# Two decoder layers on one core: high-part and low-part matmuls of a weight tile, k tile by k tile in place of one run after the other

## The chip, the cores and the metric

The kernel runs on one core of one Trainium2 chip. The metric is the device time of one execution in microseconds (us). The kernel before takes 2217.95 us, the median of three runs (2217.54 to 2218.45). A profile is one execution recorded by the hardware profiler; its times count from the start of the span, which is the time from the first to the last instruction.

## The reference

A trunk of two decoder layers works on 256 tokens of 2048 features, in float32:

```python
for layer in range(2):
    h = rmsnorm(x, mix_norm[layer])
    x = x + (sliding_window_attention(h, ...) if layer == 0 else rglru_block(h, ...))
    h = rmsnorm(x, ffn_norm[layer])
    x = x + conv_ffn(h, ...)
```

- Attention: 32 query heads and 8 key/value heads of 64, a window of 128, normed q and k, a learned sink in the softmax, then the output projection (2048 x 2048).
- RG-LRU: an input projection (2048 x 4096) into an x branch and a y branch; a causal convolution over 4 positions and block-diagonal gates (8 blocks of 256) on the x branch; a linear recurrence over the tokens; its result times gelu(y); the output projection (2048 x 2048).
- ConvFFN: `u = h @ w_up` (2048 x 12288), a causal convolution over 3 positions, `gelu(g) * v` of the two halves of `u`, and `@ w_down` (6144 x 2048). Both layers end with one; with their 288 of the 376 weight chunks they are most of the work.

## The kernel before, in words

**Layout.** Activations stay on chip, transposed: features on the 128 partitions, the 256 tokens along the free axis. `x` is the residual stream, `h` its normed form, in 16 "k tiles" of 128 features.

**Two parts of every operand.** A float32 number is split exactly into a high and a low part of type float32r. A product is hi*hi + hi*lo + lo*hi, accumulated in float32 in PSUM. With a weight's high part stationary, TensorE streams both parts of the activation, `[x_hi | x_lo]`, 512 columns; with its low part stationary, it streams `x_hi` alone, 256 columns, which are added to the second half of the same PSUM bank. So each k tile of each output tile needs one 512-column matmul (`mm_hi`, line 183) and one 256-column matmul (`mm_lo`, line 189), each with its own load of a 128 x 128 weight tile. Before the change `mm_hi` runs over all k tiles of an output tile first, and `mm_lo` after it.

**The stream of weights.** Weights come from HBM once, in 376 chunks of 1 MiB (128 x 2048), in the order of their use. Each has three buffers' worth of room at each stage: `raw` (as loaded), `hi` and `lo`. `advance()` (line 122) is called once per chunk, after that chunk's matmuls: it issues the transfer of a later chunk on SyncE's queue (line 102), has ScalarE cast a chunk's high part (line 109) and VectorE subtract to get its low part (line 117). A high buffer is free again when the last matmul that reads it is done, a raw buffer when the low split has read it.

**The stages, in order**, by the name of the PSUM tile:
- `pk`, `pv`, `pq`: the attention's projections. `attend()` weaves the steps of the attention between the high matmuls of a q tile.
- `po`: output projection, 16 output tiles. The first two go together, because the last two k tiles of `ao` come late; lines 605 to 608 run these k tiles alternately, high then low, one output tile after the other.
- `pu` and `pd`: the ConvFFN's up and down projection, in two halves of 24 pairs of `pu` tiles (one pair: a tile of `g` and one of `v`) and 8 pairs of `pd` tiles. One `pd` chunk holds 8 k tiles for two output tiles, so a run there has 8 matmuls, not 16.
- `px`, `py`: x and y branch of the RG-LRU's input projection, 20 and 12 output tiles. Behind `px` pairs follow the gate matmuls `g`. During `py`, the steps of the recurrence (`decay`, `coef`, `root`, `recur`, `proj`, `gated`, `zsplit`) are placed by hand on ScalarE, VectorE and GpSimd by the tables `before` and `after`; they produce `z`.
- `pr`: the RG-LRU's output projection from `z`, 16 output tiles; then the second ConvFFN.

**Late operands.** Where a stage's last two k tiles come late (the first pair of `pu`, `px` and `pr`), `late_pair()` (line 214) runs 14 k tiles of both output tiles first, then `mid()` (the norm's matmuls), then the last two.

**Epilogues.** Each is a generator, whose steps (`step(pend)`) are issued while the next tile's matmuls run: ScalarE copies one half of the bank, VectorE adds the other, and so on. PSUM has three double-bank buffers for these tiles.

**Order of the work.** All engines execute in the written order (a manual schedule); the waits between them follow from the tiles that they write and read.

Of the kernel before, what the change touches and what calls it, by code (L numbers as in the profile page):

```python
# [25 lines left out]
P = 128  # L26
D = 2048
T = 256
KD = D // P
# [11 lines left out]
def trunk(ctx, tc, xT, wq, wk, wv, wo, win, wg, wout, wup, wdn, mixg, ffng, kqg, sinks,  # L41
# [85 lines left out]
    def use():  # L127
        """The next chunk's parts."""
        c = st["use"]
        st["use"] += 1  # L130
        return his.pop(c), los.pop(c)
# [5 lines left out]
    def step(g):  # L137
        """Runs a generator to its next yield."""
        if g is not None:
            next(g, None)  # L140

# [1 line left out]
    def split_x(dst, src, gains, k):  # L143
        """dst[:, k] = the two parts of src * gain (src [P, T])."""
        act.activation(out=dst[:, k, 0, :], in_=src, func=AF.Copy, scale=gains[:, k:k + 1])
        dve.scalar_tensor_tensor(out=dst[:, k, 1, :], in0=src, scalar=gains[:, k:k + 1],
                                 in1=f(dst[:, k, 0, :]), op0=ALU.mult, op1=ALU.subtract)

    def stat(src, first):
        """sqa += src * src (src [P, 2, T])."""  # L150
        if first:
            pool.tensor_tensor(out=sqa, in0=src, in1=src, op=ALU.mult)
        else:
            pool.tensor_tensor(out=sqt, in0=src, in1=src, op=ALU.mult)  # L154
            pool.tensor_tensor(out=sqa, in0=sqa, in1=sqt, op=ALU.add)
# [5 lines left out]
    def rsqrt1(y, v):  # L161
        """A first guess of v ** -0.5."""
        act.activation(out=y, in_=v, func=AF.Ln)
        act.activation(out=y, in_=y, func=AF.Exp, scale=-0.5)

    def rsqrt2(y, v, tmp):
        """One Newton step towards v ** -0.5."""
        dve.tensor_tensor(out=tmp, in0=v, in1=y, op=ALU.mult)
        dve.scalar_tensor_tensor(out=tmp, in0=tmp, scalar=-0.5, in1=y, op0=ALU.mult, op1=ALU.mult)
        dve.scalar_tensor_tensor(out=y, in0=tmp, scalar=1.5, in1=y, op0=ALU.add, op1=ALU.mult)  # L170
# [20 lines left out]

    def x_epi(ps, d, n, gains, tp, out_=None, tag="xt"):
        """x's tiles d .. d + n take the product in ps [P, n, 512]; then h's, or the output's."""
        t = tp.tile([P, n, T], F32, tag=tag, name=f"xt{st['use']}")
        xs = x[:, d:d + n, :]
        for i in ([slice(0, n)] if out_ is None else [slice(i, i + 1) for i in range(n)]):
            dve.tensor_tensor(out=t[:, i], in0=ps[:, i, 0:T], in1=xs[:, i], op=ALU.add)  # L197
            dve.tensor_tensor(out=xs[:, i], in0=ps[:, i, T:], in1=t[:, i], op=ALU.add)  # L198
            if out_ is not None:
                nc.sync.dma_start(out=out_[:, d:d + n, :][:, i], in_=xs[:, i])  # L200
        if out_ is not None:
            return
        yield
        if gains is None:
            return
        for i in range(d, d + n):
            split_x(h, x[:, i, :], gains, i)
        yield
        if n == 2:
            stat(xs, d == 0)  # L210
        elif d % 2:
            stat(x[:, d - 1:d + 1, :], d == 1)

    def late_pair(ps, rhs, mid=None):
        """Two output tiles whose operand's last two k-tiles come late."""
        parts = [use(), use()]
        for i, (hi, lo) in enumerate(parts):
            mm_hi(ps[:, i], hi, rhs, rng(0, KD - 2))
            mm_lo(ps[:, i], lo, rhs, rng(0, KD - 2), stop=False)
        advance()  # L220
        if mid:
            mid()
        for i, (hi, lo) in enumerate(parts):
            mm_hi(ps[:, i], hi, rhs, rng(KD - 2, KD), start=False)
            mm_lo(ps[:, i], lo, rhs, rng(KD - 2, KD))
        advance()

    def softplus():
        """sp = softplus(-lam) = max(-lam, 0) + log1p(e), e = exp(-|lam|), by the series of
        log1p(e) = 2 artanh(z), z = e / (2 + e) <= 1/3."""  # L230
# [41 lines left out]
    # ================= attention =================  # L272
    with ExitStack() as ph:
# [35 lines left out]
        # key j of two blocks is seen from query i when i < j <= i + 128  # L309
# [69 lines left out]
        def kv_norm():  # L379
            """The first norm's factor along the free axis and along the partitions."""  # L380
            ps = psT.tile([P, 512], F32, tag="pT", name="pn")
            norm_pe(ps[:, 0:T])
            pc = psT.tile([P, 512], F32, tag="pT", name="pc")
            for b in range(2):
                for i in range(2):
                    pe.matmul(pc[:, b:b + 1], lhsT=sqa[:, i, b * P:(b + 1) * P], rhs=ones[:, 0:1],
                              start=i == 0, stop=i == 1)
            dve.tensor_scalar(out=cb, in0=ps[:, 0:T], scalar1=1.0 / D, scalar2=EPS, op0=ALU.mult, op1=ALU.add)
            dve.tensor_scalar(out=cb, in0=cb, scalar1=EPS, scalar2=None, op0=ALU.mult)
            dve.tensor_scalar(out=rcv, in0=pc[:, 0:2], scalar1=1.0 / D, scalar2=EPS, op0=ALU.mult, op1=ALU.add)  # L390
            dve.tensor_scalar(out=cc, in0=rcv.unsqueeze(2).to_broadcast([P, 2, 2]), scalar1=EPS, scalar2=None, op0=ALU.mult)
            rsqrt(rc, rcv, rct)
# [85 lines left out]
        def softmax(j, S):  # L478
            # column 2 * b + a: block b, head a
# [55 lines left out]
        def values(j):  # L535
# [3 lines left out]
            for b in range(2):  # L539
                # (key block, slice of the transposed probabilities)  # L540
# [15 lines left out]
        def attend(j, ps, hi, lo, rhs, nk):  # L556
            """One output tile's products over nk of its k-tiles; between them the steps of the
            attention of the query tiles j - 1 and j - 2."""
# [58 lines left out]
        for d in range(2, 16):  # L617
            hi, lo = use()
            ps = pj.tile([P, 512], F32, tag="pj", name=f"po{d}")
            mm_hi(ps, hi, ao, rng(0, KD))  # L620
            mm_lo(ps, lo, ao, rng(0, KD))
# [16 lines left out]
    # ================= ConvFFN =================  # L638
    def ffn(layer, nxt):
        with ExitStack() as ph:  # L640
# [29 lines left out]
            for half in range(2):  # L670
                for m in range(KH):
# [4 lines left out]
                    else:  # L676
                        for i in range(2):
                            hi, lo = use()
                            mm_hi(ps[:, i], hi, h, rng(0, KD))
                            mm_lo(ps[:, i], lo, h, rng(0, KD))  # L680
# [5 lines left out]
                for dp in range(8):  # L686
                    ps = mm.tile([P, 2, 512], F32, tag="mm", name=f"pd{layer}_{half}_{dp}")
                    for c in range(3):
                        hi, lo = use()
                        ks = [(kk, 8 * c + kk) for kk in range(8)]  # L690
                        for i in range(2):
                            mm_hi(ps[:, i], hi, g, ks, off=i * P, n=2 * P, start=c == 0)
                            mm_lo(ps[:, i], lo, g, ks, off=i * P, n=2 * P, stop=c == 2)
# [9 lines left out]
    # ================= RG-LRU =================  # L703
    with ExitStack() as ph:
# [6 lines left out]
        def projected(ps, n, eng):  # L711
            """A pair of output tiles: the two halves of the bank added, times the norm's factor."""
# [8 lines left out]
        with ExitStack() as px:  # L721
# [48 lines left out]
            def gates_rest(n, ps):  # L770
                """r (kept in a), i * x (in u), and t = tanh(4 sp r)."""
# [23 lines left out]
            for n in range(10):  # L795
# [3 lines left out]
                else:  # L799
                    rest = None  # L800
                    for i in range(2):
                        hi, lo = use()
                        mm_hi(ps[:, i], hi, h, rng(0, KD))
                        mm_lo(ps[:, i], lo, h, rng(0, KD))
# [21 lines left out]
        # a = exp(-8 sp r) = 1 - t (1 + a), and sqrt(1 - a a) = sqrt(t) (1 + a)  # L826
# [37 lines left out]
        # (n, i): what follows the products of tile i of the y projection's pair n, before the stream  # L864
        # moves on and after it
# [21 lines left out]
        for n in range(2, 8):  # L887
            ps = mm.tile([P, 2, 512], F32, tag="mm", name=f"py{n}")
            yps.append(ps)
            for i in range(2):  # L890
                hi, lo = use()
                mm_hi(ps[:, i], hi, h, rng(0, KD))
                mm_lo(ps[:, i], lo, h, rng(0, KD))
# [5 lines left out]
        for n in range(8):  # L899
# [7 lines left out]
            else:  # L907
                for i in range(2):
                    hi, lo = use()
                    mm_hi(ps[:, i], hi, z, rng(0, KD))  # L910
                    mm_lo(ps[:, i], lo, z, rng(0, KD))
# [12 lines left out]
def _layout(inp):  # L924
    import numpy as np

    def cols(w):
        """[K, N] -> [N / 128, 128, K / 128, 128]: chunk per 128 columns, rows on partitions."""
# [3 lines left out]
    def vec(v):  # L932
        """[..., n * 128] -> [128, ..., n]"""
# [49 lines left out]
```

## Time and profile before

| | |
|---|---|
| median of the runs | 2217.95 us (2217.54 to 2218.45) |
| span of the profiled execution | 2215.8 us |
| TensorE matmul (PE) busy | 2185.9 us, 99% of the span |
| TensorE weight load (PEld) busy | 1921.5 us, 87% |
| VectorE (DVE) busy | 1568.6 us, 71% |
| ScalarE (ACT) busy | 1142.7 us, 52% |
| GpSimd (POOL) busy | 186.7 us, 8% |
| mean granted TensorE clock | 0.995 |
| HBM read | 401.06 MB, 182 GB/s with the writes over the span |

The profiled execution has no time of its own beside the span; the runs' times lie 1.7 to 2.7 us above it, which is what stands around the first and last instruction.

How to read it. A line of the groups gives the kernel line, the engine, the operation, output <- inputs by the program's names, the shape and the count, then busy time and mean duration of one, then the idle time of the engine just before them. A row of the timeline gives start, length, engine, line and operation, the count of merged instructions (xN), and in brackets the idle time before it and what ended it. Consecutive matmuls overlap in the record, since an end is modelled as including the way through the array; so the pace is read from starts, not from durations.

### The profile page before, as it was taken

Reading aid. Unit: us, or ns where it says so; the run is one execution under the profiler, and the core shown is the slowest. Engines: PE = TensorE matmul, PEld = TensorE weight load, DVE = VectorE, ACT = ScalarE, POOL = GpSimd, SP = SyncE. Lnnn points to the kernel's source line nnn. Section 1 sums busy time; section 2 is a strip of 40 time slices with the busy share of each in tenths; the row PEclk is TensorE's granted clock in tenths of the full one; section 3 lists DMA queues with packets and bytes.
Section 4 is the critical chain, followed back from the end, with each engine's and each line's share of the span. In section 5 each row is a group of like instructions: output and inputs, shape, how many; then the busy total and the mean of one; then the engine's idle time right before and its main releaser. Section 6 shows DMA issues by size and latency. Waiting matters only on the chain.

```text
span 2215.8 us, 30701 instructions
## 1 busy us (share of the span) xinstructions
PE 2185.9 (99%) x12656; PEld 1921.5 (87%) x12656; DVE 1568.6 (71%) x1862; ACT 1142.7 (52%) x1400; POOL 186.7 (8%) x155
## 2 busy tenths in 40 slices
PE   7999999999999999999999979999999999999999
PEld 6888888888888888888889868888888888888888
DVE  7877767777644777776677787777776457777654
ACT  4777445555433555553366744455554335555432
POOL 4122220000000000002200143200000000000000
PEclk9999999999999999999999999999999999999999
DMA  6333555555555555555465445555555555555543
GB/s 218 134 116 116 189 189 208 191 190 190 190 186 194 187 192 191 191 190 189 163 223 176 163 152 194 186 191 190 190 190 192 190 188 190 190 190 190 190 190 133
DMA packets 61053, 405.15 MB, mean 183 GB/s; under 512 B 7537, under 2 KB 9969, under 8 KB 13169
## 3 DMA queue, kind: packets, MB, share of 16 engines
q1 hardware_dynamic: 60912, 403.19, 51.3%
q8 instruction: 99, 1.62, 0.3%
q14 instruction: 42, 0.34, 0.0%
HBM read 401.06 MB, written 2.10 MB: 182 GB/s over the span
## 4 chain that ended last, share of the span: by engine, by line
PE 93%; DVE 3%; ACT 2%; issue 1%; POOL 1%; DMA 0%; SPq 0%; DVEq 0%; ACTq 0%
PE pu L183 32%; PE pu L189 16%; PE pd L183 16%; PE pd L189 8%; PE px L183 3%; PE po L183 3%; PE pr L183 3%; PE pq L183 2%; PE px L189 2%; PE pr L189 1%; PE po L189 1%; PE pq L189 1%; PE O L544 1%; DVE lo L117 1%; POOL ps L717 1%
## 5 line engine op out<-in xcount | busy, mean ns | idle before, releaser
L117 DVE TENSOR_TENSOR lo<-raw,hi 128x2048 fp32r<-128x2048 f32 (+1 forms) x390 | 858.1, 2200 | 223.8 <-ACT hi L109 222.6
L109 ACT CAST hi<-raw 128x2048 fp32r<-128x2048 f32 x373 | 713.0, 1912 | 386.1 <-PE pd L183 248.0
L183 PE MATMUL pu<-h,hi 128*128 128x512 f32 x3072 | 736.7, 392 | 0.0
L183 PEld LDWEIGHTS pu<-h,hi 128*128 128x128 f32 x3072 | 563.0, 188 | 111.2
L189 PEld LDWEIGHTS pu<-h,lo 128*128 128x128 f32 x3072 | 383.5, 188 | 16.4
L189 PE MATMUL pu<-h,lo 128*128 128x256 f32 x3072 | 387.0, 278 | 0.0
L183 PE MATMUL pd<-g,hi 128*128 128x512 f32 x1536 | 384.6, 392 | 0.0
L183 PEld LDWEIGHTS pd<-g,hi 128*128 128x128 f32 x1536 | 276.2, 189 | 49.4
L189 PEld LDWEIGHTS pd<-g,lo 128*128 128x128 f32 x1536 | 209.6, 190 | 14.9
L189 PE MATMUL pd<-g,lo 128*128 128x256 f32 x1536 | 214.2, 282 | 0.0
L666 ACT CAST g<-us 128x256 fp32r<-128x256 f32 x96 | 39.0, 406 | 280.7 <-DVE us L665 280.7
L659 DVE SCALAR_TENSOR_TENSOR uy<-us,fw,uy 128x255 f32<-128x255 f32 (+1 forms) x384 | 176.7, 481 | 6.8
L651 DVE TENSOR_TENSOR us<-pu,ua 128x512 f32<-128x512 f32 x96 | 66.4, 692 | 154.7 <-ACT ua L650 154.6
L650 ACT COPY ua<-pu 128x512 f32<-128x512 f32 x96 | 56.3, 587 | 143.4 <-PE pu L189 143.4
L656 ACT ACTIVATE uy<-us,fb,fw 128x256 f32<-128x256 f32 x192 | 104.8, 596 | 2.7 <-DVE us L652 2.7
L197 DVE TENSOR_TENSOR xt<-pd,x 128x512 f32<-128x512 f32 (+1 forms) x40 | 23.3, 583 | 83.3 <-PE pd L189 83.3
L154 POOL TENSOR_TENSOR sqt<-x 128x512 f32<-128x512 f32 x28 | 64.5, 2305 | 179.1 <-DVE x L198 176.6
L183 PE MATMUL px<-h,hi 128*128 128x512 f32 x320 | 77.7, 395 | 0.0
L667 DVE TENSOR_TENSOR g<-us,g 128x256 fp32r<-128x256 f32 x96 | 40.8, 425 | 45.3 <-ACT g L666 45.3
L183 PE MATMUL pr<-z,hi 128*128 128x512 f32 x256 | 63.1, 396 | 8.8 <-DVE z L861 7.8
L183 PE MATMUL pq<-h,hi 128*128 128x512 f32 x256 | 71.3, 403 | 0.2 <-DVE vh L442 0.2
L183 PEld LDWEIGHTS px<-h,hi 128*128 128x128 f32 x320 | 58.8, 189 | 11.8
(195 smaller groups left out, 1844.2 us busy)
## 6 DMA issues: line engine op xcount, KB each, us to landing
raw<-in_wup SPq DMA_DIRECT2D x192, 1024.0 KB, 4.8
raw<-in_wdn SPq DMA_DIRECT2D x96, 1024.0 KB, 4.8
raw<-in_win SPq DMA_DIRECT2D x32, 1024.0 KB, 4.8
raw<-in_wq SPq DMA_DIRECT2D x16, 1024.0 KB, 4.7
raw<-in_wo SPq DMA_DIRECT2D x16, 1024.0 KB, 4.8
raw<-in_wout SPq DMA_DIRECT2D x16, 1024.0 KB, 4.8
raw<-in_wv SPq DMA_DIRECT2D x4, 1024.0 KB, 5.4
graw<-in_wg SPq DMA_DIRECT2D x8, 512.0 KB, 3.4
```

Of the source, the lines that this page charges most:

```text
L109: act.copy(out=his[c], in_=raws[c])
L117: dve.tensor_tensor(out=los[c][:, part], in0=raws[c][:, part], in1=f(his[c][:, part]), op=ALU.subtract)
L154: pool.tensor_tensor(out=sqt, in0=src, in1=src, op=ALU.mult)
L183: pe.matmul(ps, lhsT=hi[:, off + k * n:off + k * n + P], rhs=rhs[:, xk].rearrange("p a t -> p (a t)"), start=start and k == ks[0][0], stop ...
L189: pe.matmul(ps[:, T:], lhsT=lo[:, off + k * n:off + k * n + P], rhs=rhs[:, xk, 0, :], start=False, stop=stop and k == ks[-1][0])
L197: dve.tensor_tensor(out=t[:, i], in0=ps[:, i, 0:T], in1=xs[:, i], op=ALU.add)
L650: act.copy(out=a, in_=ps[:, :, 0:T])
L651: dve.tensor_tensor(out=s, in0=ps[:, :, T:], in1=a, op=ALU.add)
L656: act.activation(out=y[:, i, :], in_=s[:, i, :], func=AF.Identity, scale=fw[:, layer, n, 2:3], bias=fb[:, layer, n:n + 1])
L659: dve.scalar_tensor_tensor(out=y[:, i, tap:], in0=s[:, i, 0:T - tap], scalar=fw[:, layer, n, 2 - tap:3 - tap], in1=y[:, i, tap:], op0=ALU. ...
L666: act.copy(out=g[:, m, 0, :], in_=s[:, 0, :])
L667: dve.tensor_tensor(out=g[:, m, 1, :], in0=s[:, 0, :], in1=f(g[:, m, 0, :]), op=ALU.subtract)
```

## The change

A new helper, `mm_both`, calls `mm_hi` and `mm_lo` for one k tile at a time. All projections but `pk`, `pv` and `pq`, and the first two tiles of `po`, call it in place of `mm_hi` for all k tiles followed by `mm_lo` for all k tiles. The start flag stays on the first high matmul of an output tile, the stop flag on its last low one. The number of matmuls, weight loads, splits and transfers is the same, and so is their order in every queue but TensorE's. (The full diff also strips comments and docstrings, with the line numbers above the helper kept.)

```diff
+    def mm_both(ps, hi, lo, rhs, ks, off=0, n=P, start=True, stop=True):
+
+        for k in ks:
+            mm_hi(ps, hi, rhs, [k], off, n, start and k == ks[0])
+            mm_lo(ps, lo, rhs, [k], off, n, stop and k == ks[-1])
+
...
     def late_pair(ps, rhs, mid=None):
...
         for i, (hi, lo) in enumerate(parts):
-            mm_hi(ps[:, i], hi, rhs, rng(0, KD - 2))
-            mm_lo(ps[:, i], lo, rhs, rng(0, KD - 2), stop=False)
+            mm_both(ps[:, i], hi, lo, rhs, rng(0, KD - 2), stop=False)
...
         for i, (hi, lo) in enumerate(parts):
-            mm_hi(ps[:, i], hi, rhs, rng(KD - 2, KD), start=False)
-            mm_lo(ps[:, i], lo, rhs, rng(KD - 2, KD))
+            mm_both(ps[:, i], hi, lo, rhs, rng(KD - 2, KD), start=False)
...
             ps = pj.tile([P, 512], F32, tag="pj", name=f"po{d}")
-            mm_hi(ps, hi, ao, rng(0, KD))
-            mm_lo(ps, lo, ao, rng(0, KD))
+            mm_both(ps, hi, lo, ao, rng(0, KD))
...
                             hi, lo = use()
-                            mm_hi(ps[:, i], hi, h, rng(0, KD))
-                            mm_lo(ps[:, i], lo, h, rng(0, KD))
+                            mm_both(ps[:, i], hi, lo, h, rng(0, KD))
...
                         for i in range(2):
-                            mm_hi(ps[:, i], hi, g, ks, off=i * P, n=2 * P, start=c == 0)
-                            mm_lo(ps[:, i], lo, g, ks, off=i * P, n=2 * P, stop=c == 2)
+                            mm_both(ps[:, i], hi, lo, g, ks, off=i * P, n=2 * P, start=c == 0, stop=c == 2)
```

The tiles of `px`, `py` and `pr` change in the same way as the `pu` tile above.

More of the change, by code (lines that the diff above doesn't have):

```diff
@@ L802, in trunk @@
                         hi, lo = use()
-                        mm_hi(ps[:, i], hi, h, rng(0, KD))
-                        mm_lo(ps[:, i], lo, h, rng(0, KD))
+                        mm_both(ps[:, i], hi, lo, h, rng(0, KD))
                         if i == 0:
@@ L891, in trunk @@
                 hi, lo = use()
-                mm_hi(ps[:, i], hi, h, rng(0, KD))
-                mm_lo(ps[:, i], lo, h, rng(0, KD))
+                mm_both(ps[:, i], hi, lo, h, rng(0, KD))
                 run(before.get((n, i), ()))
@@ L909, in trunk @@
                     hi, lo = use()
-                    mm_hi(ps[:, i], hi, z, rng(0, KD))
-                    mm_lo(ps[:, i], lo, z, rng(0, KD))
+                    mm_both(ps[:, i], hi, lo, z, rng(0, KD))
                     step(pend)
```

## The prediction

> **What bounds the kernel now.** I read the page first: busy shares, the granted clock, the chain that ended last, the costliest groups.
>
> ```profile
> PE 2185.9 (99%) x12656; PEld 1921.5 (87%) x12656; DVE 1568.6 (71%) x1862; ACT 1142.7 (52%) x1400; POOL 186.7 (8%) x155
> ...
> PEclk9999999999999999999999999999999999999999
> ...
> PE 93%; DVE 3%; ACT 2%; issue 1%; POOL 1%; DMA 0%; SPq 0%; DVEq 0%; ACTq 0%
> ...
> L183 PE MATMUL pu<-h,hi 128*128 128x512 f32 x3072 | 736.7, 392 | 0.0
> ...
> L189 PE MATMUL pu<-h,lo 128*128 128x256 f32 x3072 | 387.0, 278 | 0.0
> ```
>
> TensorE is busy 99% of the span and carries 93% of the chain, its clock is full in every slice, and its two large groups never waited (last column 0.0). So the time is the spacing of the matmuls, start to start. The 392 and 278 ns are durations that overlap and are no spacing; that comes from the starts of whole runs, in the timeline. First, two tiles of the up projection (`pu`), sixteen high-part matmuls and sixteen low-part ones each:
>
> ```profile
> 501.70 3.84 PE L183 MATMUL pu<-h,hi 128*128 128x512 f32 x16
> ...
> 505.37 1.98 PE L189 MATMUL pu<-h,lo 128*128 128x256 f32 x16
> ...
> 507.19 3.82 PE L183 MATMUL pu<-h,hi 128*128 128x512 f32 x16
> ...
> 510.85 2.05 PE L189 MATMUL pu<-h,lo 128*128 128x256 f32 x16
> ...
> 512.73 3.84 PE L183 MATMUL pu<-h,hi 128*128 128x512 f32 x16
> ```
>
> A high matmul takes (505.37 - 501.70) / 16 = 0.229 us. A low one takes 1.82 / 16 = 0.114 in one tile and 1.88 / 16 = 0.1175 in the next. One high and one low, a "pair", cost (512.73 - 501.70) / 32 = 0.3447 us. The same for one chunk of the down projection (`pd`):
>
> ```profile
> 573.39 2.00 PE L183 MATMUL pd<-g,hi 128*128 128x512 f32 x8
> 575.22 1.12 PE L189 MATMUL pd<-g,lo 128*128 128x256 f32 x8
> 576.18 2.00 PE L183 MATMUL pd<-g,hi 128*128 128x512 f32 x8
> ...
> 578.97 0.40 PE L183 MATMUL pd<-g,hi 128*128 128x512 f32 x1
> ```
>
> Its pair costs 5.58 / 16 = 0.3488; the high ones are again 1.83 / 8 = 0.229, the low ones 0.96 / 8 = 0.120. The other four projections, as stretches that each hold whole tiles (`po` and `pr` one tile of 16 pairs, `px` without its gate matmuls and `py` two):
>
> ```profile
> 235.22:240.79 5.57, 5.57 (x34) 1.00 0.98 372
> 1334.41:1339.98 5.57, 5.57 (x35) 1.00 0.40 150
> 1253.07:1264.10 11.03, 11.03 (x66) 1.00 0.54 189
> ...
> 1137.97:1149.14 11.17, 11.17 (x66) 9.80 (x65) 8.26 (x12) 10.29 (x14) 0.00 (x0) 1.00 0.44 147
> ```
>
> `po` and `pr` 0.3481, `py` 0.3447, `px` 0.3491 us a pair.
>
> **The change part by part.** Nothing is added or removed: the same weight loads, matmuls, splits and transfers. TensorE runs matmuls in the written order, so what changes is each one's neighbour, when a low part is first wanted (one matmul after the high part, not sixteen), and when a high part is last used (one before the tile's end).
>
> *The pace of an alternating stream.* From the loops, the pairs that change are 192 tiles x 16 = 3072 in `pu`, 96 chunks x 16 = 1536 in `pd`, and 14, 20, 12 and 16 tiles x 16 = 224, 320, 192 and 256 in `po`, `px`, `py` and `pr`; 5600 in all. `pk`, `pq` and the first two `po` tiles stay. The trace before has no long alternating stream, but it has short ones. The first two `po` tiles already go high, low, high, low for their last two k tiles:
>
> ```profile
> 229.18 0.28 PE L189 MATMUL po<-ao,lo 128*128 128x256 f32 x1
> 229.29 0.40 PE L183 MATMUL po<-ao,hi 128*128 128x512 f32 x1
> 229.53 0.28 PE L189 MATMUL po<-ao,lo 128*128 128x256 f32 x1
> 229.64 1.78 PE L183 MATMUL po<-ao,hi 128*128 128x512 f32 x7
> ...
> 229.87 0.40 PE L183 MATMUL po<-ao,hi 128*128 128x512 f32 x1
> ```
>
> From low to low 0.35, from high to high 0.35, from the last low to the end of the high one after it 0.34. The pairs of tiles whose operand comes late go two high, two low:
>
> ```profile
> 318.93 0.62 PE L183 MATMUL pu<-h,hi 128*128 128x512 f32 x2
> ...
> 319.62 0.62 PE L183 MATMUL pu<-h,hi 128*128 128x512 f32 x2
> ...
> 1333.02 0.63 PE L183 MATMUL pr<-z,hi 128*128 128x512 f32 x2
> ...
> 1333.71 0.63 PE L183 MATMUL pr<-z,hi 128*128 128x512 f32 x2
> ...
> 1334.41 3.82 PE L183 MATMUL pr<-z,hi 128*128 128x512 f32 x16
> ```
>
> That is 0.69 / 2 = 0.345, 0.69 / 2 = 0.345 and 0.70 / 2 = 0.350. The six readings have a mean of 0.3467 us, with 0.340 and 0.351 as their ends (the starts are rounded to 0.01). I take 0.3467 for all 5600. Against today's: `pu` +0.0020 x 3072 = +6.1; `pd` -0.0021 x 1536 = -3.2; `po` and `pr` -0.0014 x 480 = -0.7; `px` -0.0024 x 320 = -0.8; `py` +0.0020 x 192 = +0.4. Sum: +1.8 us.
>
> One page speaks for a gain here. The Trainium skill, page "TensorE: Matmul & The Clock Gate", section "LDWEIGHTS (loading the stationary operand)", gives a load as its columns divided by 1.2, by my estimate 107 ns for 128 columns, as long as a low matmul and half a high one; a run of low matmuls would then be paced by loads, and alternating would give every second load a long matmul to hide under. The trace agrees in part (low runs at 0.114 to 0.120, though a high matmul's load under one low matmul has no more cover than before); its result is the first rival below.
>
> *A low part that is not ready yet.* Two places are tight. Splits and tiles, counted in program order, give the first three of these rows; two pieces of the chain of waits, the wait for `z` and the clock behind it follow:
>
> ```profile
> 228.82 2.29 DVE L117 TENSOR_TENSOR lo<-raw,hi 128x2048 fp32r<-128x2048 f32 x1
> ...
> 1280.62 3.36 PE L183 MATMUL py<-h,hi 128*128 128x512 f32 x14
> 1281.02 2.29 DVE L117 TENSOR_TENSOR lo<-raw,hi 128x2048 fp32r<-128x2048 f32 x1
> ...
> 1281.02 2.29 DVE lo L117
> ...
> 1289.66 1.71 DVE z L861
> ...
> 1324.38 1.22 PE L183 MATMUL pr<-z,hi 128*128 128x512 f32 x2 [5.38 <-DVE z L861]
> 1325.40 2.90 PE L189 MATMUL pr<-z,lo 128*128 128x256 f32 x14
> 1328.14 3.36 PE L183 MATMUL pr<-z,hi 128*128 128x512 f32 x14
> ...
> 1324.38:1328.14 3.76, 3.76 (x16) 0.54 0.55 233
> ```
>
> The third `po` tile starts at 229.64 and its low part is ready at 231.11: TensorE issues one high matmul (0.23), then waits 231.11 - 229.87 = 1.24 us, with the fifteen other high ones queued behind the waiting low one. TensorE is the bound afterwards, so this is +1.2 us.
>
> The last three `py` pairs are the other place: the tile that starts at 1280.62 has its low part at 1283.31, which costs 2.7 - 0.23 = 2.5 us of wait, and by the same count the low parts of the five tiles behind it end 2.0 to 3.2 us after their tile's start, 13.0 us together. But in this stage TensorE does not set the end. The chain runs through VectorE (its low split and its `z`, above), and TensorE sits idle for 5.38 us before 1324.38. If each tile begins at the later of its high part and the tile before, and its second matmul at the later of its low part, I arrive at k tile 12 of the first `pr` tile at 1320.0, still 4.4 us early. Cost: nothing, under the cover of that idle time; up to 14 us if the cover were gone (the third rival). There is even a gain: before, fourteen low matmuls stand behind the wait for `z`, from 1325.40 to 1328.14; after, twelve of them have gone ahead into the idle time. At the half clock they ran at (granted 0.54; 2.74 / 14 = 0.196 each) they would save 2.3 us, but the half-clock stretch after the idle time stays as long and falls on other matmuls, so I take the full-clock price, 12 x 0.117 = -1.4 us.
>
> *High buffers freed later.* ScalarE's next high split waits for the release of a buffer three chunks older, up to 15 low matmuls (1.8 us) later than now:
>
> ```profile
> 511.04 1.91 ACT L109 CAST hi<-raw 128x2048 fp32r<-128x2048 f32 x1 [0.27 <-PE pu L183]
> ...
> 513.85 2.29 DVE L117 TENSOR_TENSOR lo<-raw,hi 128x2048 fp32r<-128x2048 f32 x1
> ```
>
> Here the tile's high run ends at 510.85 and the split follows at 511.04. Moved to about 512.9 it ends at 514.8; queued behind it are the gelu and the next epilogue copy on ScalarE (whose operand ends at 512.73 + 16 x 0.3447 = 518.2), and the low split on VectorE, which ends near 517.1 instead of 516.1. That chunk is used three tiles after 507.19, at 523.7. The transfer into the raw buffer that the low split frees starts 1 us later and has the same margin. Cost: nothing; without that margin it would be at most 1 us a tile.
>
> Sum against the profiled execution: 1.8 + 1.2 - 1.4 = +1.6 us on a span of 2215.8, so 2217.4. The median of the runs shown is 2217.95, 2.15 more than that span; I carry this along: **2219.5 us**.
>
> **The rivals.**
>
> *Faster: the low runs are held up by loads, and alternating frees them.* For it: the low spacing differs between 0.114 and 0.120 while all have the same shape. Against it: each matmul still has one load beside it. If each low matmul takes the best 0.1138 and the high ones stay at 0.229, the pairs lose 0.0018 in `pu` and about 0.0056 elsewhere: -5.5 - 8.6 - 2.9 - 1.9 - 0.3 = -19 us, 2199. If the pair goes to the lowest reading, 0.340, it is -14.4 - 13.5 - 3.9 - 2.9 - 0.9 = -36 us, 2182.
>
> *Slower: each change of part costs.* The mechanism is a small slip of TensorE when a low matmul follows a high one or a high one a low one, which today is paid once a tile and then sixteen times. For it: the first two alternating readings are 0.35. Against it: the `pu` run boundaries show no step. At 0.351 the pairs add 19.4 + 3.4 + 1.4 + 0.6 + 1.2 = +26 us, 2244. It decides from 0.3477 up, where the sum passes what a measurement can tell.
>
> *Slower: the late low parts count.* If the stalls of the last `py` tiles delay the chain that makes `z` (through buffers released later), 2.7 + 13.0 us less 0.23 for each of six, some 14 us, come on top: 2233. It decides from the point where TensorE reaches k tile 12 after 1324.4, 4.4 us later than I have it. Against it: the chain before 1324 runs over the other engines.
>
> *The change does nothing*, because TensorE's spacing depends only on shapes: 2218. It can't be told from the forecast.
>
> **How the numbers follow.** The forecast and "does nothing" together have 0.43; low matmuls freed 0.16, all the way to 0.340 0.07; a cost for each change of part 0.28; late low parts that count 0.06. What a measurement of this kernel can tell from no change is about 0.2%, 4.4 us. Faster by more: 0.16 + 0.07 = 0.23; slower by more: 0.28 + 0.06 = 0.34; within: 0.43. The forecast's own range is 2214 to 2223. For 8 in 10 the range takes in the freed low matmuls (2199) and the slower reading (2244), and leaves out the lowest pair: 2199 to 2245.
>
> **What would show it.** In the timeline high and low must alternate one by one within a `pu` tile. Two `pu` tiles that start 11.09 us apart (32 x 0.3467) say that the forecast's pace is right; 10.9 or less says freed loads; 11.2 or more a cost for each change. `pd` should fall from 5.58 to 5.55 us a chunk. The third `po` tile should show a wait of about 1.2 us for L117 on VectorE, the last `py` tiles waits of 1 to 3 us for the same, and the wait for `z` before k tile 12 of `pr` should still end near 1324 plus what is gained or lost before it. If that last one moves by itself, my cover was wrong; if `pu` and `pd` move in different directions by more than the sum says, one pace for all was wrong.

## The result, and the profile after

The changed kernel takes 2246.55 us, the median of four runs (2244.05 to 2248.72), against 2218.2 us for the kernel before: a ratio of 1.0129, 95% interval 1.0115 to 1.0143. It is slower by 28 us, 1.3%. The profiled execution spans 2244.6 us, 28.8 more than before.

The page of the kernel after (columns as before: busy time, mean duration, idle time before):

```profile
PE 2216.0 (99%) x12656; PEld 1932.3 (86%) x12656; DVE 1576.5 (70%) x1862; ACT 1129.9 (50%) x1400; POOL 183.6 (8%) x155
...
L183 PE MATMUL pu<-h,hi 128*128 128x512 f32 x3072 | 1086.0, 396 | 0.0
...
L189 PE MATMUL pu<-h,lo 128*128 128x256 f32 x3072 | 866.3, 282 | 0.0
```

The bound is the same, TensorE, with the same instructions and no wait in the large groups. Their busy times (1086.0 and 866.3 us) now overlap and can't be added up, since high and low matmuls alternate. So the pace is read again from lengths, now of whole stretches of stages between two starts (columns: stretch, length, TensorE busy and its instructions, granted clock, DMA share, GB/s). First the kernel after: a `pd` stretch of 384 pairs, a `pu` stretch of 768, another `pd`.

```profile
581.27:714.39 133.12, 133.12 (x770) 1.00 0.54 190
714.39:985.75 271.36, 271.36 (x1538) 1.00 0.52 186
985.75:1121.43 135.68, 135.68 (x770) 1.00 0.51 182
```

The same three in the kernel before:

```profile
573.39:707.46 134.07, 134.07 (x770) 1.00 0.54 189
707.46:972.41 264.95, 264.95 (x1538) 1.00 0.54 191
972.41:1106.49 134.08, 134.08 (x771) 1.00 0.52 183
```

`pu` went from 264.95 / 768 = 0.3450 to 271.36 / 768 = 0.3533 us a pair, 6.4 us a stretch and 25.6 us in the four of them. `pd` went from 0.3491 to 133.12 / 384 = 0.3467 in one stretch and to 135.68 / 384 = 0.3533 in another, although the two run the same code on tiles at the same places. The timelines show what repeats. `pu` after:

```profile
500.00 0.39 PE L183 MATMUL pu<-h,hi 128*128 128x512 f32 x1
...
500.35 0.40 PE L183 MATMUL pu<-h,hi 128*128 128x512 f32 x1
...
500.71 0.40 PE L183 MATMUL pu<-h,hi 128*128 128x512 f32 x1
...
501.06 0.39 PE L183 MATMUL pu<-h,hi 128*128 128x512 f32 x1
```

The first `pd` stretch after:

```profile
589.94 0.39 PE L183 MATMUL pd<-g,hi 128*128 128x512 f32 x1
590.17 0.28 PE L189 MATMUL pd<-g,lo 128*128 128x256 f32 x1
590.28 0.39 PE L183 MATMUL pd<-g,hi 128*128 128x512 f32 x1
...
590.63 0.39 PE L183 MATMUL pd<-g,hi 128*128 128x512 f32 x1
```

In `pd` each pair takes 0.3467. In `pu` three pairs repeat after 1.06 us. These values are whole numbers of steps of 6.67 ns (52 steps a pair; 159 for three, 53 a pair). The step is inferred from the distances between the paces that recur, here 0.3533 - 0.3467. The pattern locks: behind their first few tiles these stretches keep one pace to their end. `h` alone does not fix it: `py`, which streams the same `h` as `pu`, runs at 0.3489 (64 pairs in 22.33 us, from 1257.34 to 1279.67).

### The profile page after: what moved, and what is told of

Its sections match the earlier page's. It is cut to its first block, busy times and chain, and to the rows that moved or that the text cites. A ratio compares the mean times of both kernels' runs of the same rounds, so it can differ in the third digit from the quotient of the medians.

```text
span 2244.6 us, 30701 instructions
## 1 busy us (share of the span) xinstructions
PE 2216.0 (99%) x12656; PEld 1932.3 (86%) x12656; DVE 1576.5 (70%) x1862; ACT 1129.9 (50%) x1400; POOL 183.6 (8%) x155
## 4 chain that ended last, share of the span: by engine, by line
PE 93%; DVE 3%; ACT 2%; issue 1%; POOL 1%; DMA 0%; SPq 0%; DVEq 0%; ACTq 0%
PE pu L183 32%; PE pu L189 16%; PE pd L183 16%; PE pd L189 8%; PE px L183 3%; PE po L183 3%; PE pr L183 3%; PE pq L183 2%; PE px L189 2%; PE po L189 1%; PE pr L189 1%; PE pq L189 1%; PE O L548 1%; DVE lo L117 1%; POOL ps L718 1%
## 5 line engine op out<-in xcount | busy, mean ns | idle before, releaser
L183 PE MATMUL pu<-h,hi 128*128 128x512 f32 x3072 | 1086.0, 396 | 0.0
L189 PE MATMUL pu<-h,lo 128*128 128x256 f32 x3072 | 866.3, 282 | 0.0
L189 PEld LDWEIGHTS pu<-h,lo 128*128 128x128 f32 x3072 | 576.9, 188 | 0.1
L183 PE MATMUL pd<-g,hi 128*128 128x512 f32 x1536 | 537.8, 395 | 0.0
L189 PE MATMUL pd<-g,lo 128*128 128x256 f32 x1536 | 430.7, 280 | 0.0
L189 PEld LDWEIGHTS pd<-g,lo 128*128 128x128 f32 x1536 | 290.2, 189 | 0.0
L183 PE MATMUL px<-h,hi 128*128 128x512 f32 x320 | 112.7, 395 | 0.0
L189 PE MATMUL px<-h,lo 128*128 128x256 f32 x320 | 89.8, 281 | 0.0
L183 PE MATMUL po<-ao,hi 128*128 128x512 f32 x256 | 88.2, 397 | 1.1 <-DVE ao L558 1.1
L189 PE MATMUL pr<-z,lo 128*128 128x256 f32 x256 | 72.6, 283 | 1.1 <-DVE lo L117 1.1
```

The source lines that it names most:

```text
L183: pe.matmul(ps, lhsT=hi[:, off + k * n:off + k * n + P], rhs=rhs[:, xk].rearrange("p a t -> p (a t)"), start=start and k == ks[0][0], stop ...
L189: pe.matmul(ps[:, T:], lhsT=lo[:, off + k * n:off + k * n + P], rhs=rhs[:, xk, 0, :], start=False, stop=stop and k == ks[-1][0])
```

## The experiments

Theory A: alternating matmuls fall into a repeating cycle on a grid of 6.67 ns, and which cycle depends on the order and on the point of the grid at which a stretch is entered. Theory B: each change between high and low costs a fixed slip. Theory C: late low parts and buffers freed late made the loss. Theory D: the accumulation in PSUM did. A time without an interval is that of one execution.

**Groups of two and of four.**

```diff
-        for k in ks:
-            mm_hi(ps, hi, rhs, [k], off, n, start and k == ks[0])
-            mm_lo(ps, lo, rhs, [k], off, n, stop and k == ks[-1])
+        for i in range(0, len(ks), 2):        # 4 in the second run
+            mm_hi(ps, hi, rhs, ks[i:i + 2], off, n, start and i == 0)
+            mm_lo(ps, lo, rhs, ks[i:i + 2], off, n, stop and i + 2 >= len(ks))
```

> Edit: two high matmuls, then the two low ones of the same k tiles, in place of one and one; half as many changes of part. Pace of a pair (one high, one low) in the changed kernel: pu 0.3533 us everywhere; pd 0.3467 in two of its four stretches and 0.3533 in the other two; before: pu 0.3448, pd 0.3492. Theory A (a repeating pattern locks to a grid of 6.67 ns, and which whole number of steps it needs depends on the order and on the point of the grid at which it starts): no proportion to the number of changes; some stretch of tiles with a pace that is a multiple of 6.67 ns over its cycle, 0.340 to 0.3467 in pu as in the late pair of before (0.345), 0.345 to 0.350 in pd; span 2205 to 2225 us. Theory B (each change of part costs a fixed slip, 8.5 ns a pair in pu at one change pair per k tile): half the loss, pu 0.349, span about 2230 us. Theory C (late low parts and buffers freed late made the loss): pu and pd as in the changed kernel, span 2244.

> Edit: four high matmuls, then their four low ones. Theory A: again a pace of its own in each stretch, not a quarter of the loss; 0.340 to 0.3533, span 2195 to 2245. Theory B: a quarter of the loss, pu 0.3469, span about 2223. Theory C: 2244.

Measured: 2217.08 and 2220.79 us, the kernel before 2217.32 beside them. The second `pu` stretch of the groups of two, then of four:

```profile
709.75:974.74 264.99, 264.99 (x1538) 1.00 0.54 191
```

```profile
708.96:974.55 265.59, 265.59 (x1538) 1.00 0.54 190
```

With half the changes the whole loss of `pu` is gone (0.3450), with a quarter of them it is 0.3458, worse than with half. Nothing goes in proportion to the changes, so B falls. C falls too: with groups of two, high buffers are freed and low parts wanted nearly as late and as early as with one and one.

**One extra matmul.**

```diff
                             hi, lo = use()
+                            if m == 1 and i == 0:
+                                pe.matmul(ps[:, i, 0:512], lhsT=hi[:, 0:P], rhs=h[:, 0].rearrange("p a t -> p (a t)")[:, 0:512],
+                                          start=True, stop=True)
                             mm_both(ps[:, i], hi, lo, h, rng(0, KD))
...
                         hi, lo = use()
+                        if dp == 0 and c == 0:
+                            pe.matmul(ps[:, 0, 0:512], lhsT=hi[:, 0:P], rhs=g[:, 0].rearrange("p a t -> p (a t)")[:, 0:512],
+                                      start=True, stop=True)
```

> Edit: the changed kernel, and one more 512-column matmul (the first one of a tile, run twice, its first result overwritten) once at the second pair of pu tiles of each half and once at the first pd tile of each half: 8 extra matmuls in all, about 8 x 0.23 = 1.8 us. Theory A: it shifts the point of the grid at which the stretch starts, so in at least one of the pd stretches (0.3467, 0.3533, 0.3533, 0.3467 in order) the pace of all 384 pairs changes by 6.67 ns (2.6 us a stretch), and perhaps in pu (768 pairs, 5.1 us). Theory B and C: the pace of each stretch stays what it is, span + 1.8 us.

Measured: 2247.70 us. Its first `pd` and second `pu` stretch, each with one matmul more:

```profile
582.51:718.42 135.91, 135.91 (x772) 1.00 0.53 186
718.42:986.74 268.32, 268.32 (x1540) 1.00 0.53 189
```

Less 0.23 us for the extra matmul, `pd` went from 133.12 to 135.68 (0.3467 to 0.3533) and `pu` from 271.36 to 268.09 (0.3533 to 0.3491). One matmul moved the pace of hundreds of pairs behind it, by whole steps in `pd`. Of the three theories left only A allows this. The move did not come everywhere: two of the four `pd` stretches and two of the four `pu` stretches changed, and the first `pu` stretch, which has its extra matmul too, kept its 0.3533. Whether the point of the grid decides, as A says, or something else in what runs ahead of a stretch, no run separates.

**Low matmuls into the first half of the bank.**

```diff
-            pe.matmul(ps[:, T:], lhsT=lo[:, off + k * n:off + k * n + P], rhs=rhs[:, xk, 0, :],
+            pe.matmul(ps[:, :T], lhsT=lo[:, off + k * n:off + k * n + P], rhs=rhs[:, xk, 0, :],
```

> Edit: in every projection the low matmul adds to the first half of its PSUM bank, not the second (the sum of the two halves that the epilogue forms is the same). Theory D (the slip comes from the accumulation: a low matmul adds to columns that the high one wrote last, and the next high one begins on the other half): the distances change from 256 columns each to 256 and 0, so the pace changes everywhere, by 5 ns or more. Theory A: the pace stays on the same few values, 0.3467 and 0.3533, and pu at 0.3533; span 2240 to 2247.

Measured: 2236.49 us. Its first `pd`, second `pu`, then the third `pd` and the fourth `pu`:

```profile
581.31:714.43 133.12, 133.12 (x770) 1.00 0.53 190
714.43:985.79 271.36, 271.36 (x1538) 1.00 0.52 186
1695.98:1829.10 133.12, 133.12 (x770) 1.00 0.54 190
1829.10:2097.05 267.95, 267.95 (x1538) 1.00 0.53 189
```

From 309 to 1121 us every `pu` and `pd` stretch has the length that it has in the changed kernel, so D falls. After the waits of the `py` and `pr` stages the stretches are on other cycles (`pu` 0.3489, `pd` 0.3467), and that alone makes the 10 us.

**The place of the tiles.** Before the change, `pu` and `pr` use the same shapes, but their low runs are spaced 0.114 to 0.1175 and 0.120. What differs is where the streamed tile lies. Start addresses in SBUF, in bytes per partition, and their distance to the high and low parts modulo 256 (buffers of one kind are 8192 apart):

```
hi 86592   lo 111168   h 17536 (64)   ao 160320 (0)   g 135744 (0)   z 195136 (0)
```

Theory E: these distances set the cycle. Two edits of the kernel before (the first also of the changed one and of the groups of two) move either all but `h` or `h` alone:

```diff
-    sp = per.tile([P, KD], F32, name="sp")
+    sp = nt[:, 0:KD]
...
+    padh = per.tile([P, 16], F32, name="padh")     # second edit only
     h = per.tile([P, KD, 2, T], F32R, name="h")
```

> Edit to the kernel before: a 64-byte tile (sp) is moved into another one's space, so that every tile behind it lies 64 bytes lower. Before, h starts at a multiple of 128 bytes and the weights' parts, g, ao and z at 64 past one; now all start at a multiple of 128. Theory E (the grid's cycle depends on where the two operands lie, relative to each other or to 128 bytes): the pace of pd, po and pr, today 0.3492 and 0.3480 us a pair, and of pu, 0.3450, changes, and pd and pu now have one and the same pace; if it is the lowest spacings seen (0.2267 high, 0.1133 low) a pair is 0.340, span 2180; if the highest (0.2333 and 0.120), 0.3533 and span 2255. Theory A without the address (only order and starting point matter): pu 0.3450 and pd 0.3492 as before, span 2216.

> The same edit to the changed kernel. Theory E: pu leaves 0.3533 and pd and pu share their set of values; if a pair locks at 0.340, span about 2180, if at 0.3467, 2217. Without the address: pu 0.3533, pd 0.3467 or 0.3533, span 2240 to 2248.

> The same edit to the kernel with groups of two. Theory E: pu (0.3451) and pd (0.3484) change and become equal, between 0.340 and 0.3533. Without the address: as in group2, span 2215.

> Edit to the kernel before: sp's 64 bytes are put ahead of h, so h too starts 64 past a multiple of 128, like the weights' parts, g, ao and z, which stay where they are. Theory E: pu, px and py now run like pd, po and pr: low runs at 0.120, a pair at 0.348 to 0.349 and not 0.345, so span up by about 3072 x 0.003 = 9 us. If pu equals pd here and in align_before too, only the relative place counts. Without the address: pu 0.3450, span 2216.

Measured: 2238.62 us (ratio 1.0096, 1.0079 to 1.0113), 2244.42 us (1.0121, 1.0106 to 1.0136), 2227.37 and 2239.36 us. `pd` and `pu` of the first and of the last:

```profile
577.27:711.36 134.09, 134.09 (x770) 1.00 0.53 188
711.36:981.25 269.89, 269.89 (x1539) 1.00 0.53 188
```

```profile
578.22:712.30 134.08, 134.08 (x770) 1.00 0.53 188
712.30:982.19 269.89, 269.89 (x1538) 1.00 0.53 188
```

Both edits put `h` at 128 and leave `g` at 0. `pu` takes 0.3514 in both and `pd` its old 0.3491 in both, though in the first everything starts at a multiple of 128 and in the second nothing does. So the distance counts and not the place, and it costs the kernel before 21 us to have `h` 64 bytes further off. In the changed kernel `pu` moved to 0.3511 and all four `pd` stretches to 0.3533; in the groups of two `pu` rose to 0.3484. `pd` and `pu` did not become equal in the kernel before, as the expectation had it; they stand at 0 and 128. In the groups of two they did (0.3484 and 0.3483), but there only `pu` had moved.

**More distances.** Pads move `h` and, differently in the two layers, `g`:

```diff
+    gm = per.tile([P, 2, KD], F32, name="gm")      # moved ahead of h; rw in scanB_before
     h = per.tile([P, KD, 2, T], F32R, name="h")
...
+            if (16, 48)[layer]:                    # (64, 80) in scanB_before, (16, 16) in g64_before
+                gp.tile([P, (16, 48)[layer]], F32, name=f"gpad{layer}")
             g = gp.tile([P, KH, 2, T], F32R, name=f"g{layer}")
...
+        zp.tile([P, 16], F32, name="zpad")         # 80 in scanB_before
         z = zp.tile([P, KD, 2, T], F32R, name="z")
```

> Edit to the kernel before: tiles are moved by small pads, so that the distance of the streamed operand's start from the weight parts' start, modulo 512 bytes, is 192 for h (now 64), 64 for g of the first layer and 192 for g of the second (now 0), 64 for z (now 0); weights stay. Theory E (the relative place decides the pace; read so far: 0 gives 0.3492 in pd and 0.3480 in pr, 64 gives 0.3450, 128 gives 0.3514 in pu): first layer's pd and pr run at about 0.3450, first and second layer's pd differ, and pu has a pace of its own between 0.340 and 0.356. Theory E' (only h's even or odd place in 128 bytes against the weights counts, and g differs from h by its stride): pd unlike 0.3450, and pu (192) like 64, 0.3450. No address: all as before.

> The same moves in the changed kernel. Theory E: the set of paces of a stretch goes with the relative place: first layer's pd and pr (64) take the values that pu had at 64, 0.3533 or 0.3489, and not 0.3467; second layer's pd and pu (192) have values of their own. No address: pd 0.3467 or 0.3533, pu 0.3533 or 0.3489.

> As the first, with the distance 320 for h, 256 for g of the first layer, 320 for g of the second and 320 for z. Theory E: four more readings; pd of the second layer, pr and pu share one pace (all 320); if one of them is near 0.340 there is a place that saves up to 14 us in pu. If a distance of 256 repeats 0 (0.3492) and 320 repeats 64 (0.3450), what counts is modulo 256 bytes.

> Edit to the kernel before: 64 bytes of pad ahead of g in both layers and ahead of z, so that pd and pr stand at the distance of 64 bytes that pu, px and py have. Theory E: pd 0.3492 to about 0.3450 (1536 x 0.0042 = 6.4 us) and pr 0.3480 to 0.3450 (0.8 us): time about 2210.5, a version that beats both. No address: 2217.6.

Measured: 2216.76, 2256.57, 2212.28 us, and for the last 2208.60 us, a ratio of 0.9962 (0.9949 to 0.9976). In scanA_before, `pd` of the first layer (64), `pu` (192), `pd` of the second layer (192):

```profile
575.19:707.56 132.37, 132.37 (x770) 1.00 0.55 190
707.56:973.81 266.25, 266.25 (x1538) 1.00 0.54 190
1677.99:1811.11 133.12, 133.12 (x770) 1.00 0.54 189
```

In scanB_before, `pd` of the first layer (256), `pu` (320), `pd` of the second (320):

```profile
572.31:706.39 134.08, 134.08 (x771) 1.00 0.54 189
706.39:971.34 264.95, 264.95 (x1539) 1.00 0.54 191
1676.37:1808.74 132.37, 132.37 (x770) 1.00 0.54 191
```

256 repeats 0 and 320 repeats 64, so the distance counts modulo 256. In the order of the kernel before, a pair of `pu` or `pd` takes 0.3491 at 0, 0.3447 to 0.3450 at 64, 0.3514 at 128 and 0.3467 at 192. Other stages need not have the same pace at the same distance: `po` and `pr` take 0.348 at 0, and `px`, whose pairs of tiles have gate matmuls between them, 0.3491 at 64. In the alternating order no such table comes out. All stages of scanA_after stand at 0.3533, at 64 and at 192, and `po` too, which stayed at 0 and had 0.3467 in the changed kernel. Moving only `g` and `z` to 64 gives a kernel that is faster than the one before by 0.4%.

**High and low parts set apart.** In the order of the kernel before, a matmul in a run of sixteen is spaced 0.228 us (high) and 0.120 (low) at 0, in `pr`, and 0.233 and 0.114 at 192, in `pu` of scanA_before. Theory F: each matmul's spacing goes with its own distance, so that 0 from one kind of parts and 192 from the other must give 0.340 in one order and 0.3533 in the other.

```diff
     hip = ctx.enter_context(tc.tile_pool(name="hip", bufs=3))
+    padp = ctx.enter_context(tc.tile_pool(name="padp", bufs=1))
+    padp.tile([P, 16], F32, name="pad")
     lop = ctx.enter_context(tc.tile_pool(name="lop", bufs=3))    # swap: lop, pad, hip
...
-    sp = per.tile([P, KD], F32, name="sp")
+    sp = nt[:, 0:KD]
```

with `gm` ahead of `h` and 192 bytes of pad ahead of `g` and `z`.

> Edit to the kernel before: tiles are moved so that h, g and z stand 0 from the high parts and 192 from the low parts, modulo 256 bytes (today: h 64 and 64, g and z 0 and 0). Read so far in this order: at 0 and 0 the long high runs reach 0.2267 but the low ones 0.120; at 192 and 192 high 0.233 and low 0.1137. Theory F (a matmul's spacing depends on the distance of what it streams to the weights that are loaded under it, which in a run are its own kind's): high about 0.228, low 0.1137, a pair 0.342: 9 + 11 + 1.5 + 2 + 0.6 us less, time about 2194. Theory F2 (the pattern of both kinds together decides): another pace, anything from 0.3445 to 0.351, time 2207 to 2235.

> The same places in the changed kernel. There the load under a high matmul is a low part's, and under a low one a high part's. Theory F with the weights loaded under it: 192 under the high ones (0.233), 0 under the low ones (0.120): 0.3533, span 2243 or more. With the weights that the matmul itself uses: 0.340, span about 2182. Theory F2: 0.3467 to 0.3533.

> The changed kernel with the low parts' buffers ahead of the high parts', so that h, g and z stand 192 from the high parts and 0 from the low parts. Theory F with the weights loaded under it: 0 under the high matmuls (0.2267), 192 under the low ones (0.1133): a pair 0.340, span about 2182, the best of all. With the weights that the matmul itself uses: 0.3533, span 2243 or more. Theory F2: 0.3467 to 0.3533.

> The kernel before with the same places as the last one: 192 from the high parts, 0 from the low parts. Theory F: high runs 0.233, low runs 0.120, a pair 0.353, span about 2240. Theory F2: another pace.

Measured: 2217.21 us (0.9999, 0.9991 to 1.0008), 2215.86 us (0.9995, 0.9986 to 1.0004), 2237.29 us (1.0088, 1.0072 to 1.0103) and 2246.30 us. Second `pu` stretch of split_before, then, in split_after, 193 pairs of `po` and the second `pu` stretch:

```profile
707.61:973.52 265.91, 265.91 (x1538) 1.00 0.54 190
```

```profile
240.19:305.81 65.62, 65.62 (x388) 1.00 0.55 193
...
706.04:972.28 266.24, 266.24 (x1538) 1.00 0.54 190
```

swap_after (64 pairs of `py`, then the same `pu` stretch), and the `pu` stretch of swap_before:

```profile
1252.41:1274.17 21.76, 21.76 (x130) 1.00 0.44 152
...
715.69:984.49 268.80, 268.80 (x1538) 1.00 0.53 188
```

```profile
714.81:985.21 270.40, 270.40 (x1538) 1.00 0.53 187
```

A pair of `pu` takes 0.3462, 0.3467, 0.3500 and 0.3521. F gave 0.342 for the first, and 0.340 or 0.3533 for the second and third; only the fourth comes near its 0.353. So F falls. In the old order it holds for the high runs (0.228 at 0 in split_before, 0.234 at 192 in swap_before) and not for the low ones (0.118 in both). In swap_after all stages but `po` stand at the same two distances and still have three paces: 0.3500 in `pu` and `pd`, 0.3533 in `pr`, and 0.3400, one of F's two values, in `py`. So the places and the order together don't fix the cycle either. But split_after loses nothing against the kernel before, in the alternating order, and holds one stage nobody had aimed at. `ao` had kept its place from the low parts, 0, and now lay 64 from the high ones, and `po` ran at 0.3400, 51 steps; no stretch of any kernel here is quicker.

**All stages at that place.** `h`, `g` and `z` too are put 64 from the high parts and 0 from the low ones: the pad between the pools and `sp` as in split_after, `gm` and `sp4` ahead of `h`, and no other pads.

> The changed kernel with h, g, z and ao all 64 bytes from the high parts and 0 from the low parts, modulo 256. One stage has stood there so far: po in split_after, 216 pairs at 0.3400 us, against 0.3467 at 0 and 192. Theory H (the two distances together set the pace, the same in all stages): 0.340 everywhere; against split_after's 2215.9 that is 5376 x 6.67 ns = 36 us less, time about 2180. If the pace of po is its own or depends on the starting point alone: 0.3467 or 0.3533 in pu and pd, time 2215 to 2245.

> The kernel before (all high, then all low) with the same places. po stood there in split_before: 0.3494 us a pair. Theory H with the order as the third thing that counts: 0.348 to 0.351 in all stages, time 2225 to 2240, so at these places the change gains 2% or so, where at the old places it lost 1.3%. If the places alone make the gain: as fast as the run above.

Measured: the old order 2229.04 us (1.0053, 1.0038 to 1.0067). The alternating order has a median of 2196.24 us (0.9902, 0.9867 to 0.9937), but its ten runs fall into two clusters: five from 2182.19 to 2184.86 and five from 2207.62 to 2211.80. The profiled run, 2208.02 us, is of the second. Its first `pd` and second `pu` stretch, two pieces of `py` (16 pairs, then 24), and the fourth `pu` stretch:

```profile
569.61:700.17 130.56, 130.56 (x770) 1.00 0.55 194
700.17:961.29 261.12, 261.12 (x1538) 1.00 0.55 194
1270.96:1276.40 5.44, 5.44 (x33) 1.00 0.51 173
1286.84:1295.24 8.40, 8.40 (x49) 1.00 0.68 236
1798.52:2067.32 268.80, 268.80 (x1539) 1.00 0.54 188
```

The old order, second `pu` stretch:

```profile
709.70:977.23 267.53, 267.53 (x1538) 1.00 0.54 189
```

Up to the `py` stage all runs at 0.3400. There TensorE waits three times for low parts; behind the first of these waits the pace is 0.3400 again, behind the last it is 0.3500, and after the wait for `z` in `pr` everything runs at 0.3500. The 2304 pairs of the second ConvFFN and the 256 of `pr` at 10 ns are 25.6 us; the medians of the clusters (2182.70 and 2208.53) lie 25.8 apart. No run of the quick cluster has a profile, so that it stays at 0.3400 to the end is worked out and not seen. Order and place act together: here the alternating order wins 1.5% against the old one by the medians (2196.24 to 2229.04), where at the old places it lost 1.3%. The 2196.24 lies between the clusters, where no run does; the quick one is 2.1% below the old order, the other 0.9%.

## Why the prediction was wrong, point by point

- **The bound** (TensorE, paced by spacing): right.
- **"I take 0.3467 for all 5600":** this is the step that failed. It was a mean of six short readings of two or three matmuls, taken as one pace for all. `pd` gave 0.3467 in two stretches and 0.3533 in two, `po` 0.3467, `pr` 0.3533, and `pu`, which carries the sum, 0.3533. `px` and `py` were at 0.349. The term, forecast at +1.8 us, measured 25.6 in `pu` and 1.3 in `pd`. From the start of `px` to the end of `pr` the span grew by 0.4 us and in `po` by 2.7 (below), while `po` began 1.3 us earlier, which stays unexplained. Together these are 28.7 of the 28.8 us.

  Two things were wrong in the step. First, the six readings were taken from starts rounded to 0.01 us; by the trace's own starts, which are kept in nanoseconds, they are 0.344 to 0.352 with a mean of 0.3484, which would have made the term some +11 us. Second, a few matmuls behind another kind of run need not have the spacing of a long alternating stream: 0.3533 lies above all six. And since one execution holds `pd` at both 0.3467 and 0.3533, no short stretch of the trace before could have told which cycle `pu` would lock to. That a pace repeats in cycles, and that more than one is open to a stage, the runs show; why `pu` took this one stays open.
- **The rival "each change of part costs"** forecast 2244 us at 0.351, close to the result, and the prediction's sign for it came true (two `pu` tiles 11.3 us apart, where 11.2 or more was to say so). That was luck. Its mechanism fell: with groups of two the cost is not half but gone.
- **The freed low matmuls:** the only gains in pace were 0.0024 us a pair for `pd`, in half of its stretches, and 0.001 for `po`. The Trainium skill, page "TensorE: Matmul & The Clock Gate", section "Back-to-back issue gap", gives an isolated gap of N / 2.4 + 2.5 ns; my estimate from it is 215.8 + 109.2 = 325 ns a pair. The lowest pace of any stretch in these runs is 340.0 ns, so the measurement decides against it here.
- **A low part not ready in `po`,** +1.2 us: it is there, 1.1 us. But this stage grew by 2.7 us (95.68 to 98.41) although its time per pair fell. The stage before, then after:

```profile
211.91:307.59 95.68, 94.61 (x556) 1.00 0.53 189
```

```profile
210.64:309.05 98.41, 96.23 (x557) 0.98 0.51 182
```

  The waits of TensorE in the kernel after (what waits, for what: idle us, how often, longest us):

```profile
PE pr L183 <- DVE z L861: 4.0, 1, 4.0
PE py L189 <- DVE lo L117: 3.1, 3, 1.9
PE pr L189 <- DVE lo L117: 1.1, 1, 1.1
PE po L189 <- DVE lo L117: 1.1, 1, 1.1
PE po L183 <- DVE ao L558: 1.1, 1, 1.1
```

  A stretch behind the wait for the low part, of the same kernel, then the 4.25 us behind the same wait in the kernel with low matmuls into the first half of the bank (columns as for the stretches above):

```profile
230.42:233.82 3.40, 3.40 (x13) 0.50 0.80 282
```

```profile
231.55:235.80 4.25, 4.25 (x24) 1.00 0.77 262
```

  The granted clock is 0.50 for 3.4 us, and the loss half of it, 1.7 us. Two waits of 1.1 us, 1.2 us apart, stand ahead of it. They do not decide it alone: all eight kernels with one and one have both waits, and in four of their eight traces, the second one above among them, the clock stays full. So the change makes these 1.7 us possible, and that this execution has them is chance. The Trainium skill, same page, section "Part 1: The HAM clock gate (the "warmup" mystery)", has a window of 3.4 us and two states, full and half; the first of the two rows agrees with both.

- **Late low parts in `py` cost nothing, and `pr` gains 1.4 us:** both right. TensorE does wait there (3.1 and 1.1 us, above), but from the start of `py` to the end of the wait for `z` it is 82.63 us after and 82.42 before, and from there to the end of `pr` 87.73 after and 87.96 before, with a pace that costs some 1.3 us more. The two stretches after, then before:

```profile
1257.34:1339.97 82.63, 74.34 (x411) 0.98 0.44 155
1339.97:1427.70 87.73, 87.73 (x489) 0.98 0.54 191
```

```profile
1241.96:1324.38 82.42, 70.82 (x398) 0.96 0.45 156
1324.38:1412.34 87.96, 87.96 (x500) 0.98 0.54 194
```

- **High buffers freed later cost nothing:** right. TensorE waits for no high part in the kernel after.

## What to carry to other kernels

When TensorE is the bound, read the spacing of its matmuls over long stretches, and take a difference of one or two per cent between stages with the same shapes as a reason to look at where the streamed tile lies against the weights: moving a tile by 64 bytes changed `pu` by up to 1.9%, nearly as much as the order of the matmuls did (2.4%). Judge an order only together with the places of its tiles, and run it often enough to see whether it has two times. A few matmuls on either side of a boundary don't tell the pace of a pattern that has not run yet.

## What the runs showed of the hardware that was not expected

- The paces of locked stretches lie on a grid: 0.3400, 0.3467 and 0.3533 us are 51, 52 and 53 steps of 6.67 ns; 0.3489 and 0.3511 are 157 and 158 steps for three pairs, and 0.3500 is 52.5.
- One program can hold two cycles for the same stage, tiles and order: `pd` at 0.3467 and 0.3533 in one execution, and whole runs of one kernel at 2182 to 2185 or at 2208 to 2212 us. Behind one extra matmul, or a wait, a stretch can stand in another cycle.
- The distance of the streamed operand from the weights modulo 256 bytes changes the pace: in the old order from 0.3447 to 0.3514, in the alternating one down to 0.3400, where `po` came out at 64 from the high parts and 0 from the low ones in both kernels that had it there. In the alternating order a place allows several cycles. Why a pair of distances has the cycles that it has stays open; no run looked at it, and none varied the other traffic to and from SBUF (the DMA share is 0.51 to 0.55 in all the `pu` and `pd` stretches above).
